# Reciprocal roots of a two-layer encoder trunk: a root on ScalarE and a reciprocal on VectorE instead of logarithm and exponential

## The chip, the cores and the metric

One core of a Trainium2 chip runs the whole program. The metric is the device time of one execution in microseconds. TensorE (PE) multiplies matrices, VectorE (DVE) and ScalarE (ACT) do the elementwise work, GpSimd (POOL) does some of it, and SyncE's queue (SP) issues most of the transfers. ScalarE evaluates its functions from tables; where the next function needs another table, the program has an ACT_TABLE_LOAD instruction on ScalarE ahead of it.

## What is computed

The input is 512 frames of 1024 features. Each of two layers is a SwiGLU block, a mixer block and a second SwiGLU block; one more normalisation ends the trunk. The places that need a reciprocal root are these (the rest of the reference is cut away):

```
_rmsnorm(x, g):              x * rsqrt(mean(x*x) + 1e-6) * g        # ahead of each block, and at the end: 7
_head_standardize(y, eps):   (y - mu) * rsqrt(var + eps)            # eps 64e-5 for RWKV-7, 1e-5 for mLSTM
_rwkv7_mixer:                kk = k * k_k
                             kk = kk / max(sqrt(sum(kk*kk)), 1e-12)
layer:  h += 0.5 * swiglu(rmsnorm(h)) ; h += W_out(sig(g_a) * P_a(rwkv7(xn)) + sig(g_b) * P_b(mlstm(xn)))
        h += 0.5 * swiglu(rmsnorm(h))
```

## The kernel before

Features lie on the 128 partitions and the 512 frames along the free dimension. A product of 32-bit precision is made of three TensorE passes: weights and inputs are split into a rounded high part (on ScalarE, L424 for weights) and a remainder (on VectorE, L425), and lines L460 to L462 multiply high by high, high by low and low by high. Weights stream from memory through SyncE's queue; a tile of 1024 columns is used as two halves of 512.

A SwiGLU block (`ffn`) projects 22 pairs of tiles and then eight output tiles. Its normalisation is not applied to the input: `norm` computes `rstd` from the summed squares `acc` while the first projection runs, and L541 multiplies the product by it afterwards. While the eight output tiles of a block are made, a callback (`spill`, `ready` or, at the end of the program, `scaled`) prepares the next block's input tile by tile and adds its squares to `acc`.

A mixer block (`mixers`) runs under a class `Weave`, which writes out TensorE's order by hand from estimated times: generators for the RWKV-7 heads (four pairs, `rwkv`), the mLSTM heads (four, `mlstm_head`) and the shared projections (`common`) take turns. The order of the instructions on ScalarE, VectorE and GpSimd is made by the scheduler of the framework from its own estimates; each engine then works its own list strictly in order. `common` begins with a projection (`misc`) and the norm; L571 multiplies by `rstd`, and two further products (L926, L930) wait for what comes out of that chain.

The reciprocal root is `rsqrt` (L512 and L513): a logarithm and then an exponential of minus one half of it, both on ScalarE. It is called from `norm` (7 times, 128x512), from `mlstm_head` at L814 (8 times, 128x4) and from `rwkv_gated` (8 times, 128x512, on the tile `gn`, which is `acc`). `rwkv_in` does the same by hand at L957 and L958 (8 times, 128x512): there the sum is first scaled by 65536 inside the logarithm, so the result is a 256th of the root, and the factor of 256 sits in a table of columns `k256` that GpSimd fills near the start. That makes 31 roots. The functions that need a table elsewhere are Silu (L543, SwiGLU), Tanh (which also makes the sigmoids) and Exp in the mixers, and one logarithm per layer at L708. Copies, casts and squares need no table of their own.

Of the kernel before, what the change touches and what calls it, by code (L numbers as in the profile page):

```python
# [11 lines left out]
F32 = mybir.dt.float32  # L12
F32R = mybir.dt.float32r
AF = mybir.ActivationFunctionType
ALU = mybir.AluOpType
# [3 lines left out]
P = 128  # L19
D = 1024  # L20
T = 512
L = 2
FF = 2816
KD = D // P
# [304 lines left out]
class Trunk:  # L329
    def __init__(self, ctx, tc, a, out):  # L330
        self.tc, self.nc, self.a, self.out = tc, tc.nc, a, out
        pool = lambda n, b, **k: ctx.enter_context(tc.tile_pool(name=n, bufs=b, **k))
        self.pw = pool("weights", 3)
        self.pt = pool("tmp", 2)
        self.pmm = pool("mm", 3, space=PSUM)
        self.pmx = pool("mx", 5, space=PSUM)
        self.pd = pool("dram", 1, space=DRAM)
        self.keep = Scope(tc)
        nc = self.nc
        k = self.keep.tile  # L340
        self.xh = k((P, KD, T), F32R, "xh")
        self.xl = k((P, KD, T), F32R, "xl")
        self.rstd = k((P, T), F32, "rstd")
        self.acc = k((P, T), F32, "acc")
        self.cst = k((P, 4, P), F32, "cst")
        self.sel = k((P, 7, P), F32R, "sel")
        self.big = k((P, 512), F32, "big")
        self.fin = k((P, KD), F32, "fin")
        self.tid = k((P, 8, 16), F32, "tid")
        self.vec = [k((P, NCOL), F32, f"vec{l}") for l in range(L)]  # L350
        self.half = [k((P, NCOL), F32, f"half{l}") for l in range(L)]
        self.k256 = [k((P, 4), F32, f"k256_{l}") for l in range(L)]
        self.eps = k((P, 4), F32, "eps")
        self.onemu = [k((P, 15), F32, f"onemu{l}") for l in range(L)]

        k((P, 96), F32, "pad")
        self.sq, self.sl = (k((P, 512), F32R, n) for n in ("sq", "sl"))
        self.ld = [k((P, 512), F32, f"ld{i}") for i in range(2)]
        self.residual()
        for i, e in enumerate((RMS_EPS, GN_EPS, LN_EPS)):  # L360
            nc.gpsimd.memset(self.eps[:, i : i + 1], e)
        nc.scalar.copy(out=self.eps[:, 3:4], in_=self.eps[:, 0:1])
        nc.sync.dma_start(out=self.vec[0], in_=a["vec"][0])
        self.ident = self.cst[:, 0, :]
        dram = lambda n, k, s: [self.pd.tile(s, F32, name=f"{n}{i}", tag=f"{n}{i}") for i in range(k)]
        self.vfirst = dram("vfirst", 4, [P, T])
        self.bonus = dram("bonus", 4, [P, T])
        self.yd = dram("yd", 8, [P, T])
        self.hd = dram("hd", KD, [P, T])
        self.mxd = dram("mxd", 4, [64, 16, 16])  # L370
        self.gd = dram("gd", 16, [P, T])
        self.zd = dram("zd", 4, [P, 8, 16])

    def constants(self):

        nc, a = self.nc, self.a
        nc.sync.dma_start(out=self.vec[1], in_=a["vec"][1])
        nc.sync.dma_start(out=self.big, in_=a["big"])
        nc.sync.dma_start(out=self.fin, in_=a["fin"])
        nc.sync.dma_start(out=self.tid, in_=a["tid"])  # L380
        for l in range(L):
            nc.gpsimd.tensor_scalar(out=self.half[l], in0=self.vec[l], scalar1=0.5, scalar2=None, op0=ALU.mult)
        raw = self.pw.tile([P, KD * P], F32, name="wraw", tag="wraw", bufs=2)
        nc.sync.dma_start(out=raw[:, 0 : 7 * P], in_=a["sel"].rearrange("p a b -> p (a b)"))
        nc.scalar.copy(out=self.sel.rearrange("p a b -> p (a b)"), in_=raw[:, 0 : 7 * P])
        for l in range(L):
            nc.gpsimd.tensor_scalar(out=self.k256[l], in0=self.cols(l, "k_k"), scalar1=256.0, scalar2=None, op0=ALU.mult)
            s0 = _COLS["mu_misc"][0]
            nc.gpsimd.tensor_scalar(out=self.onemu[l], in0=self.vec[l][:, s0 : s0 + 15], scalar1=-1.0, scalar2=1.0, op0=ALU.mult, op1=ALU.add)

# [116 lines left out]
            eng = nc.vector if i == KD - 1 else nc.gpsimd  # L507
            eng.tensor_tensor(out=self.acc, in0=self.acc, in1=sq, op=ALU.add)  # L508

    def rsqrt(self, out, in_, eps, scale=1.0):  # L510
        nc = self.nc
        nc.scalar.activation(out=out, in_=in_, func=AF.Ln, bias=eps, scale=scale)  # L512
        nc.scalar.activation(out=out, in_=out, func=AF.Exp, scale=-0.5)  # L513

    def norm(self, last=None):
        nc = self.nc
        ps = self.mx()
        nc.tensor.matmul(ps, lhsT=self.cst[:, 1, :], rhs=self.acc, start=True, stop=last is None)
        if last is not None:
            nc.tensor.matmul(ps, lhsT=self.cst[:, 1, :], rhs=last, start=False, stop=True)  # L520
        self.rsqrt(self.rstd, ps, self.eps[:, 0:1])

    def ffn(self, l, m, done, first=None):
        nc = self.nc
# [247 lines left out]
    def mlstm_head(self, h):  # L772
        nc, l, wv = self.nc, self.l, self.wv
# [4 lines left out]
        for i in range(4):  # L778
# [4 lines left out]
            ps = self.mx()  # L783
            nc.tensor.matmul(ps[:, :n], lhsT=qk[:, 1, P * i : P * i + P], rhs=qk[:, 0, P * i :], start=True, stop=True)  # L784
            wv.pe(4 * n / 2400.0 + 0.25 * (i == 0))
            p = pt[i]
# [7 lines left out]
        s, hv = self.m_sm, pt[0].rearrange("p (j c) -> p j c", j=4)  # L794
# [16 lines left out]

        nc.vector.tensor_tensor(out=s[:, :, 8:10], in0=s[:, :, 8:10], in1=s[:, :, 1:2].broadcast_to([P, 4, 2]), op=ALU.mult)
        nc.vector.tensor_tensor(out=s[:, :, 9:10], in0=s[:, :, 9:10], in1=s[:, :, 1:2], op=ALU.mult)
        self.rsqrt(s[:, :, 10:11], s[:, :, 9:10], self.eps[:, 2:3])  # L814
        nc.vector.tensor_tensor(out=s[:, :, 1:2], in0=s[:, :, 1:2], in1=s[:, :, 10:11], op=ALU.mult)
        nc.vector.scalar_tensor_tensor(out=s[:, :, 8:9], in0=s[:, :, 8:9], scalar=-1.0, in1=s[:, :, 10:11], op0=ALU.mult, op1=ALU.mult)
        for j in range(4):
# [98 lines left out]
    def rwkv_in(self, p):  # L916

        nc, l, src, mats, wa, zm, wv = self.nc, self.l, self.src, self.mats, self.r_wa, self.zm, self.wv
# [6 lines left out]
        ps = self.mx()  # L925
# [3 lines left out]
        ps = self.mx()  # L929
# [23 lines left out]
        ps = self.sums(0)  # L953
        wv.pe(0.5)
        wv.free("halves")
        nc.vector.tensor_scalar(out=kk, in0=ps, scalar1=1e-24, scalar2=None, op0=ALU.max)
        nc.scalar.activation(out=kk, in_=kk, func=AF.Ln, scale=65536.0)  # L957
        nc.scalar.activation(out=kk, in_=kk, func=AF.Exp, scale=-0.5)  # L958
        self.shifted(rz, "mu_r", p, r)
        nc.vector.scalar_tensor_tensor(out=kk, in0=k, scalar=self.k256[l][:, p : p + 1], in1=kk, op0=ALU.mult, op1=ALU.mult)  # L960
        nc.vector.tensor_tensor(out=a3[:, :, 1:CH], in0=k3[:, :, 1:CH], in1=d3[:, :, 0 : CH - 1], op=ALU.mult)
        nc.gpsimd.tensor_copy(out=a3[:, :, 0:1], in_=k3[:, :, 0:1])
        nc.vector.scalar_tensor_tensor(out=bk[:, :, 0, :], in0=bk[:, :, 0, :], scalar=0.5, in1=k3, op0=ALU.mult, op1=ALU.mult)
# [224 lines left out]
    def rwkv_gated(self, p):  # L1188

        nc, l, mats, sg, gn, wv = self.nc, self.l, self.mats, self.r_sg, self.acc, self.wv  # L1190
        chunks = lambda x: x.rearrange("p (c t) -> p c t", c=NC)
        y = self.r_set[p % 2][0][:, :, 0, :]
        b = self.ld[0]
        nc.sync.dma_start(out=b, in_=self.bonus[p])
        yield "lock", "halves"
        self.halve(y)
        yield "at", wv.mark(2.3, 1.5)
        ps = self.sums(2)
        wv.pe(0.5)
        wv.free("halves")  # L1200
        nc.vector.tensor_tensor(out=y, in0=y, in1=chunks(ps), op=ALU.subtract)
        nc.scalar.activation(out=chunks(gn), in_=y, func=AF.Square)
        yield "lock", "halves"
        self.halve(gn)
        yield "at", wv.mark(3.2, 1.5)
        ps = self.sums(2)
        wv.pe(0.5)
        wv.free("halves")
        self.rsqrt(gn, ps, self.eps[:, 1:2])
        nc.vector.tensor_tensor(out=y, in0=y, in1=chunks(gn), op=ALU.mult)  # L1210
        nc.scalar.activation(out=y, in_=y, func=AF.Identity, scale=self.col(l, "gn_w", p), bias=self.col(l, "gn_b", p))
        nc.gpsimd.tensor_tensor(out=y, in0=y, in1=chunks(b), op=ALU.add)
        yield "at", wv.mark(6.0, 0.8)
        yield "flag", "common"
        ps = self.mx()
        F = slice(P * p, P * p + P)
        nc.tensor.matmul(ps, lhsT=mats[:, 1, F], rhs=sg, start=True, stop=False)
        lw, lx = self.low[0]
        nc.tensor.matmul(ps, lhsT=lw[:, F], rhs=lx, start=False, stop=True)
        nc.vector.tensor_tensor(out=y, in0=chunks(ps), in1=y, op=ALU.mult)  # L1220
        wv.pe(0.7)
        wv.mark(0.7, 0.7)
        nc.sync.dma_start(out=chunks(self.yd[p]), in_=y)

    def run(self):
# [12 lines left out]
        def spill(i, l):  # L1238
            self.feed(i, self.col(l, "gm", i))
            self.squares(i)  # L1240
            nc.sync.dma_start(out=self.hd[i], in_=self.h[:, i, :])

        def ready(i, l, name):
# [3 lines left out]
        def scaled(i):  # L1247

            if i < KD - 1:
                self.squares(i)  # L1250
            else:
                self.last = self.tmp("t1", 1)
                nc.scalar.activation(out=self.last, in_=self.h[:, i, :], func=AF.Square)
            nc.gpsimd.tensor_scalar(out=self.h[:, i, :], in0=self.h[:, i, :], scalar1=self.fin[:, i : i + 1], scalar2=None, op0=ALU.mult)
# [25 lines left out]
```

## Time and profile before

| | |
|---|---|
| time, median of 3 runs | 2444.64 us (2443.34 to 2445.88) |
| the profiled execution: its own time | 2444.26 us |
| its span in the trace | 2442.6 us (1.66 us lie around it) |
| busy: PE / DVE / ACT / POOL | 98% / 54% / 43% / 5% |
| chain of work that ended last: PE / DVE / ACT | 88% / 6% / 3% |
| granted TensorE clock, mean | 0.993 of full speed |
| moved by DMA | 256.13 MB, 105 GB/s on average |

The span runs from the first to the last instruction of the trace. Busy shares are averages over the whole program; PE's share counts matmuls whose ends are modelled, so back-to-back matmuls count as fully busy.

### The profile page before, as it was taken

To read this page: it belongs to the slowest core of one execution; us is meant where nothing else is said; L and a number is where in the kernel's file an instruction comes from. 1 tells how busy PE (TensorE), PEld (TensorE's weight loads), DVE (VectorE), ACT (ScalarE), POOL (GpSimd) and SP (SyncE) were. 2 spreads that over 40 slices of the span, in tenths; PEclk is the share of its full clock that TensorE was granted. 3 is DMA by queue.
4 is the path that set the end of the run, shared out by engine and by line. 5 is a ranking of instruction groups with operands and counts; after the bars stand their busy time and mean duration, and the time that the engine had idled before them with its cause. 6 is when DMAs were issued, how large, how long until landed. Compare 5 with 4: busy or idle time off the path is not lost.

```text
span 2442.6 us, 33611 instructions
## 1 busy us (share of the span) xinstructions
PE 2391.7 (98%) x13140; PEld 1948.9 (80%) x13140; DVE 1307.6 (54%) x2340; ACT 1054.2 (43%) x1795; POOL 112.8 (5%) x151
## 2 busy tenths in 40 slices
PE   8999998999999999999999999989999999999997
PEld 6888887787787888888888888867777878888886
DVE  5444447776766644444444444478677665444333
ACT  5333336555645443333343333365566454333322
POOL 0000010000000100000000000100000001000012
PEclk9999999999999999999999999999999999999999
DMA  4223342322344422323333223423223444222332
GB/s 157 95 97 101 109 121 79 112 75 78 103 151 138 139 95 97 101 93 95 98 97 102 95 93 113 134 71 95 83 87 104 137 150 135 95 95 95 96 99 82
DMA packets 116799, 256.13 MB, mean 105 GB/s; under 512 B 40064, under 2 KB 43264, under 8 KB 116640
## 3 DMA queue, kind: packets, MB, share of 16 engines
q1 hardware_dynamic: 115696, 251.30, 32.8%
q8 instruction: 103, 1.69, 0.3%
q10 hardware_dynamic: 624, 1.64, 0.2%
q0 software_dynamic: 320, 1.05, 0.1%
q14 instruction: 56, 0.46, 0.1%
HBM read 230.88 MB, written 23.07 MB: 104 GB/s over the span
## 4 chain that ended last, share of the span: by engine, by line
PE 88%; DVE 6%; ACT 3%; DMA 1%; issue 1%; SPq 0%; DVEq 0%; ACTq 0%
PE mm L460 27%; PE mm L461 27%; PE mm L462 27%; PE mx L1159 1%; DVE wlo L425 1%; PE mx L676 1%; PE mx L799 1%; PE mx L1147 1%; PE mx L784 0%; PE mx L1178 0%; PE mx L1005 0%; DVE pr L1065 0%; PE mx L1105 0%; ACT L512 0%; DVE tz L1067 0%
## 5 line engine op out<-in xcount | busy, mean ns | idle before, releaser
L424 ACT CAST whi<-wraw 128x512 fp32r<-128x512 f32 (+1 forms) x800 | 486.5, 610 | 1063.7 <-PE mm L461 984.5
L460 PE MATMUL mm<-xh,whi 128*128 128x512 f32 x2160 | 864.5, 400 | 11.2 <-ACT whi L424 11.2
L425 DVE TENSOR_TENSOR wlo<-wraw,whi 128x512 fp32r<-128x512 f32 (+1 forms) x800 | 556.2, 697 | 589.0 <-ACT whi L424 582.6
L462 PE MATMUL mm<-xh,wlo 128*128 128x512 f32 x2160 | 847.0, 392 | 5.3 <-DVE wlo L425 5.2
L461 PE MATMUL mm<-xl,whi 128*128 128x512 f32 x2160 | 845.9, 392 | 0.0
L460 PEld LDWEIGHTS mm<-xh,whi 128*128 128x128 f32 x2160 | 408.1, 189 | 105.1 <-ACT whi L424 12.3
L462 PEld LDWEIGHTS mm<-xh,wlo 128*128 128x128 f32 x2160 | 407.9, 189 | 93.1 <-DVE wlo L425 6.9
L461 PEld LDWEIGHTS mm<-xl,whi 128*128 128x128 f32 x2160 | 408.4, 189 | 82.2 <-issue 1.4
L460 PE MATMUL mm<-hh,whi 128*128 128x512 f32 x704 | 274.2, 390 | 0.0
L462 PE MATMUL mm<-hh,wlo 128*128 128x512 f32 x704 | 274.2, 390 | 0.0
L461 PE MATMUL mm<-hl,whi 128*128 128x512 f32 x704 | 274.2, 390 | 0.0
L461 PEld LDWEIGHTS mm<-hl,whi 128*128 128x128 f32 x704 | 132.3, 188 | 27.4
L462 PEld LDWEIGHTS mm<-hh,wlo 128*128 128x128 f32 x704 | 132.2, 188 | 27.3
L460 PEld LDWEIGHTS mm<-hh,whi 128*128 128x128 f32 x704 | 132.3, 188 | 27.2
L541 DVE TENSOR_TENSOR t<-mm,rstd 128x512 f32<-128x512 f32 x88 | 60.9, 692 | 139.9 <-PE mm L462 127.5
L545 DVE TENSOR_TENSOR t<-mm,t 128x512 f32<-128x512 f32 x88 | 60.9, 692 | 133.0 <-PE mm L462 130.6
L508 POOL TENSOR_TENSOR acc<-acc,t 128x512 f32<-128x512 f32 x36 | 47.9, 1329 | 1187.6 <-ACT t L506 1173.0
L543 ACT ACTIVATE t<-t 128x512 f32<-128x512 f32 x88 | 55.8, 634 | 28.9 <-DVE t L541 28.7
L487 ACT CAST hh<-t 128x512 fp32r<-128x512 f32 x88 | 54.7, 621 | 24.9 <-DVE t L545 24.9
L488 DVE TENSOR_TENSOR hl<-t,hh 128x512 fp32r<-128x512 f32 x88 | 61.0, 693 | 7.6
L495 ACT ACTIVATE xh<-h,vec 128x512 fp32r<-128x512 f32 x48 | 34.5, 724 | 45.1 <-DVE h L557 33.7
L496 DVE SCALAR_TENSOR_TENSOR xl<-h,vec,xh 128x512 fp32r<-128x512 f32 x48 | 35.8, 751 | 28.7 <-ACT xh L495 28.7
(247 smaller groups left out, 2082.7 us busy)
## 6 DMA issues: line engine op xcount, KB each, us to landing
wraw<-wi SPq DMA_DIRECT2D x94, 512.0 KB, 3.5
wraw<-f2i SPq DMA_DIRECT2D x88, 512.0 KB, 3.3
wraw<-f1i SPq DMA_DIRECT2D x86, 512.0 KB, 3.3
wraw<-f1o SPq DMA_DIRECT2D x32, 512.0 KB, 3.6
wraw<-f2o SPq DMA_DIRECT2D x32, 512.0 KB, 3.6
gd<-t SPq DMA_DIRECT2D x32, 256.0 KB, 3.4
wraw<-br SPq DMA_DIRECT2D x32, 256.0 KB, 3.1
wraw<-wo SPq DMA_DIRECT2D x16, 512.0 KB, 3.4
```

What stands on the lines that cost most here:

```text
L424: nc.scalar.copy(out=hi, in_=raw)
L425: nc.vector.tensor_tensor(out=lo, in0=raw, in1=hi.bitcast(F32), op=ALU.subtract)
L460: nc.tensor.matmul(ps, lhsT=hi, rhs=xh, start=first, stop=False)
L461: nc.tensor.matmul(ps, lhsT=hi, rhs=xl, start=False, stop=False)
L462: nc.tensor.matmul(ps, lhsT=lo, rhs=xh, start=False, stop=last)
L487: nc.scalar.copy(out=hi, in_=x)
L488: nc.vector.tensor_tensor(out=lo, in0=x, in1=hi.bitcast(F32), op=ALU.subtract)
L496: nc.vector.scalar_tensor_tensor(out=self.xl[:, i, :], in0=h, scalar=gain, in1=self.xh[:, i, :].bitcast(F32), op0=ALU.mult, op1=ALU.subtract)
L508: eng.tensor_tensor(out=self.acc, in0=self.acc, in1=sq, op=ALU.add)
L541: nc.vector.tensor_tensor(out=g, in0=pg, in1=self.rstd, op=ALU.mult)
L543: nc.scalar.activation(out=s, in_=g, func=AF.Silu)
L545: nc.vector.tensor_tensor(out=p, in0=pu, in1=s, op=ALU.mult)
```

## The change

`rsqrt` goes. A new function `root` takes the root on ScalarE (Sqrt, with the same added constant) and then the reciprocal in place on VectorE. `rwkv_in` does the same by hand, without the factor of 65536, so `k256` and its two GpSimd instructions go and L960 uses the plain column `k_k`; a filler tile grows from 96 to 112 columns. A second new function, `table`, takes the root of one column into a spare column of `eps`; it is called in `spill` (the end of the first SwiGLU block of either layer) and in `scaled` (the end of the last one) right after the squares of the last tile but one. The constant that is added, the shapes and TensorE's order are as before.

```diff
@@ trunk, constants
-        self.k256 = [k((P, 4), F32, f"k256_{l}") for l in range(L)]
-        k((P, 96), F32, "pad")
+        k((P, 112), F32, "pad")
-            nc.gpsimd.tensor_scalar(out=self.k256[l], in0=self.cols(l, "k_k"), scalar1=256.0, scalar2=None, op0=ALU.mult)
@@ rsqrt
-    def rsqrt(self, out, in_, eps, scale=1.0):
-        nc = self.nc
-        nc.scalar.activation(out=out, in_=in_, func=AF.Ln, bias=eps, scale=scale)
-        nc.scalar.activation(out=out, in_=out, func=AF.Exp, scale=-0.5)
+    def table(self):
+
+        self.nc.scalar.activation(out=self.eps[:, 3:4], in_=self.eps[:, 0:1], func=AF.Sqrt)
+
+    def root(self, out, in_, eps):
+        self.nc.scalar.activation(out=out, in_=in_, func=AF.Sqrt, bias=eps)
+        self.nc.vector.reciprocal(out=out, in_=out)
@@ norm, mlstm_head, rwkv_gated
-        self.rsqrt(self.rstd, ps, self.eps[:, 0:1])
+        self.root(self.rstd, ps, self.eps[:, 0:1])
-        self.rsqrt(s[:, :, 10:11], s[:, :, 9:10], self.eps[:, 2:3])
+        self.root(s[:, :, 10:11], s[:, :, 9:10], self.eps[:, 2:3])
-        self.rsqrt(gn, ps, self.eps[:, 1:2])
+        self.root(gn, ps, self.eps[:, 1:2])
@@ rwkv_in
-        nc.scalar.activation(out=kk, in_=kk, func=AF.Ln, scale=65536.0)
-        nc.scalar.activation(out=kk, in_=kk, func=AF.Exp, scale=-0.5)
+        nc.scalar.activation(out=kk, in_=kk, func=AF.Sqrt)
+        nc.vector.reciprocal(out=kk, in_=kk)
         self.shifted(rz, "mu_r", p, r)
-        nc.vector.scalar_tensor_tensor(out=kk, in0=k, scalar=self.k256[l][:, p : p + 1], in1=kk, op0=ALU.mult, op1=ALU.mult)
+        nc.vector.scalar_tensor_tensor(out=kk, in0=k, scalar=self.col(l, "k_k", p), in1=kk, op0=ALU.mult, op1=ALU.mult)
@@ spill, scaled: after self.squares(i)
+            if i == KD - 2:
+                self.table()
```

## Rows read from the trace of the kernel before

**Rows 1.** Page, busy time, share of the span and instructions of each engine.

```profile
PE 2391.7 (98%) x13140; PEld 1948.9 (80%) x13140; DVE 1307.6 (54%) x2340; ACT 1054.2 (43%) x1795; POOL 112.8 (5%) x151
```

**Rows 2.** Busy time by stretch: layer 1 mixer start, rest, SwiGLU; program's end.

```profile
369.00:402.00 33.00, 26.55 (x109) 20.04 (x109) 23.07 (x36) 24.21 (x35) 1.71 (x4) 0.91 0.22 72
402.00:864.00 462.00, 454.71 (x3318) 363.61 (x3317) 317.95 (x673) 249.00 (x452) 25.41 (x42) 0.99 0.36 113
864.00:1224.00 360.00, 360.00 (x1588) 298.01 (x1587) 154.12 (x227) 124.56 (x201) 8.00 (x6) 1.00 0.31 97
2418.00:2442.60 24.60, 10.19 (x41) 7.14 (x39) 7.25 (x8) 4.51 (x5) 4.49 (x3) 0.76 0.23 85
```

**Rows 3.** ScalarE's table loads by line: count, duration ns min/median/max.

```profile
L512 ACT ACT_TABLE_LOAD  x22: 1283/1283/1283, 21.9 to 2428.4; - x22
...
L513 ACT ACT_TABLE_LOAD  x22: 1283/1283/1283, 23.9 to 2430.4; - x22
...
L957 ACT ACT_TABLE_LOAD  x7: 1283/1283/1283, 411.3 to 1885.8; - x7
...
L958 ACT ACT_TABLE_LOAD  x7: 1283/1283/1283, 413.7 to 1888.7; - x7
```

**Rows 4.** VectorE instructions by line: duration ns min/median/max, then shape.

```profile
L806 DVE RECIPROCAL sm<-sm x8: 147/164/166, 466.6 to 1854.9; 128x4 f32<-128x4 f32 x8
...
L882 DVE COPY rcol<-mx x2: 152/152/152, 384.1 to 1593.3; 128x4 f32<-128x4 f32 x2
...
L541 DVE TENSOR_TENSOR t<-mm,rstd x88: 683/692/692, 25.9 to 2301.1; 128x512 f32<-128x512 f32 x88
...
L928 DVE TENSOR_SCALAR rw_w<-rw_w x8: 417/420/427, 394.0 to 1864.0; 128x512 f32<-128x512 f32 x8
...
L937 DVE TENSOR_TENSOR_SCAN rw_w<-big,rw_w x8: 1215/1224/1227, 395.7 to 1864.5; 128x512 f32<-128x512 f32 x8
```

**Rows 5.** Timeline, start of layer 1's mixer: start, duration, engine, line.

```profile
376.09 1.02 PE L518 MATMUL mx<-acc,cst 128*128 128x512 f32 x2
...
378.05 0.69 ACT L512 ACTIVATE rstd<-mx,eps 128x512 f32<-128x512 f32 x1
378.75 1.28 ACT L513 ACT_TABLE_LOAD   x1
380.05 0.63 ACT L513 ACTIVATE rstd<-rstd 128x512 f32<-128x512 f32 x1
...
380.71 0.69 DVE L571 TENSOR_TENSOR zt<-mm,rstd 128x512 f32<-128x512 f32 x1 [3.25 <-ACT rstd L513]
```

**Rows 6.** Timeline, TensorE's waits after the mixer starts, both layers.

```profile
386.88 0.69 PE L926 MATMUL mx<-wa,mats 64*128 64x512 f32 x1 [1.07 <-ACT wa L875]
...
399.81 0.80 PE L462 MATMUL mm<-xh,wlo 128*128 128x512 f32 x1 [4.51 <-DVE wlo L425]
...
1610.35 0.50 PE L460 MATMUL mm<-xh,whi 128*128 128x512 f32 x1 [3.19 <-ACT whi L424]
```

**Rows 7.** Timeline, TensorE's waits inside the mixers, both layers.

```profile
471.20 0.47 PE L1097 MATMUL mx<-mn,u 32*16 32x16 f32 x24 [0.62 <-ACT u L1092]
...
612.33 0.44 PE L676 MATMUL mx<-cst,t 128*128 128x128 f32 x2 [1.53 <-ACT t L753]
...
637.77 0.32 PE L1128 MATMUL mx<-s,mn 64*64 64x64 f32 x2 [1.77 <-ACT s L1039]
638.53 0.69 PE L1128 MATMUL mx<-s,mn 64*64 64x64 f32 x8 [0.44 <-ACT s L1039]
...
1683.77 0.39 PE L1097 MATMUL mx<-mn,u 32*16 32x16 f32 x18 [0.99 <-ACT u L1092]
```

**Rows 8.** Timeline, the end of the program.

```profile
2428.44 1.13 PE L520 MATMUL mx<-t,cst 128*128 128x512 f32 x2 [1.37 <-ACT t L1253]
...
2429.70 0.69 ACT L512 ACTIVATE rstd<-mx,eps 128x512 f32<-128x512 f32 x1
...
2432.43 1.79 DVE L1265 TENSOR_TENSOR h<-h,rstd 128x512 f32<-128x512 f32 x1 [4.76 <-ACT rstd L513]
```

More of the change, by code (lines that the diff above doesn't have):

```diff
@@ L1250, in scaled @@
                 self.squares(i)
+                if i == KD - 2:
+                    self.table()
             else:
```

## The prediction

> **What bounds the kernel now.** I read the page's busy times first: TensorE works 98% of the span [rows 1], so ScalarE and VectorE matter only where TensorE waits for them. The table by stretches says where that can be. In a SwiGLU stretch TensorE is busy for 360.00 of 360.00 us [rows 2]; the other SwiGLU stretches look the same. The four norms that stand ahead of SwiGLU blocks therefore earn nothing, whatever they cost. What is left is three kinds of places: the first 33 us of a mixer (26.55 busy, so 6.45 us lost), the rest of a mixer (7.3 us lost in 462), and the end of the program, where TensorE has finished [rows 2]. Layer 2's mixer looks like layer 1's. I then read the loads by line, and the timelines at these three kinds of places.
>
> **What one root costs now.** Nearly every root brings two table loads, one ahead of the logarithm and one ahead of the exponential: 22 + 22 + 7 + 7 = 58 loads of 1.283 us for 31 roots [rows 3]. A 128x512 root is thus some 3.9 us of ScalarE: load 1.28, logarithm 0.69, load 1.28, exponential 0.63 [rows 5].
>
> **What it costs afterwards.** Sqrt keeps the logarithm's form (one pass over the same PSUM tile with an added column), so I take its 0.69 us [rows 5]. Sqrt needs its own table, and I assume that none of Exp, Tanh or Silu lies in it; otherwise the load count would fall further. So the load ahead of the exponential does not simply vanish: the next Exp or Tanh brings its table back, later. It does vanish ahead of the four Silu blocks (which load a table anyway), at the end, and where a second root follows before any Exp or Tanh, which by ScalarE's present order is six or seven times. About 12 loads go, 15 us of ScalarE, and 23 full exponentials of 0.63 us with 8 small ones, another 16 us.
>
> **The price of the reciprocal** is the weak point, since no 128x512 reciprocal is in the trace. The nearest row is the same instruction on 128x4: 164 ns [rows 4]. A copy of 128x4 takes 152 ns. Lower bound: the cheapest 128x512 form seen, 0.42 us (L928). Upper bound: if the 12 ns above the copy all come from its four elements, each costs 3 ns more than an ordinary one. An ordinary one costs (692 - 152) / 508 = 1.06 ns, so 512 elements take 0.15 + 512 x 4.06 ns = 2.2 us. I take 0.69 us, the common price of 128x512 (L541), because at four elements the reciprocal stands within 8% of a plain copy. VectorE then gains 23 x 0.69 + 8 x 0.16 = 17 us over 1307.6 [rows 1], which is harmless as a share.
>
> The Trainium skill speaks against the change here: the page "VectorE: DVE Perf Modes", section "First, the fixed hardware budget", says that the reciprocal runs on iterative divide operations with a repeat count of 8. If that means eight cycles for each element, the change makes the kernel slower; the rival below works this out from rows. The 128x4 row speaks against that reading, though weakly, since 4 elements are few.
>
> **The start of a mixer, twice.** The norm's matmul ends at 376.09 + 1.02 = 377.11; the logarithm begins only at 378.05, because its load stands in front of it; L571, the first user of `rstd`, begins at 380.71 [rows 5]. With the table loaded during the SwiGLU stretch before (where TensorE never waits, so that 1.3 us load is covered), Sqrt begins about 0.1 us after the matmul, at 377.21, and ends at 377.90; the reciprocal ends at about 378.6, and L571 follows. That is 2.1 us earlier: 0.84 from the load moved away, 1.28 from the second load and the shorter second step. The Exp table must then come back ahead of the first Tanh (L886), but ScalarE has gaps there while VectorE makes that Tanh's input, so I charge nothing; uncovered it would cost up to 1.3. TensorE's waits after this are for the chain out of `rstd`: 1.07 us at L926, and then 4.51 us at a weight remainder which queues on VectorE behind that chain; in layer 2, 3.19 us at a weight cast [rows 6]. These ends all move with `rstd`. I count the whole 2.1 us, twice: -4.2.
>
> **The end, once.** The last matmul of the norm ends at 2428.44 + 1.13 = 2429.57, and the logarithm begins at 2429.70 [rows 8]: here the first load is almost hidden behind the matmul already, so loading it early gives no more than 0.05. From the logarithm's start to L1265 are 2.73 us; Sqrt and reciprocal take 1.38. Gain 1.4 us, all on the path: -1.4.
>
> **Inside the mixers.** I went through the waits of TensorE and kept those whose releaser stood on ScalarE right behind a root's exponential or its load. L1092 stood behind one in either layer: 0.62 and 0.99 us, saved whole. L1039 waited behind the pair of loads of a `gn` root: 1.77 + 0.44, of which I save 2.0. L753 stood behind L958: 1.53 in each layer, of which the product it copies explains all but 0.86, so 1.7 for both [rows 7]. Together 5.3 us saved. Against that stand the returning loads. The waits just listed add up to 6.9 us for 58 loads, 0.12 us a load. About twenty loads (31 roots, less the five ahead of a Silu or the end, less six or seven that another root follows) now stand at new places, ahead of some Exp or Tanh: 20 x 0.12 = 2.4 us lost. VectorE's extra 0.69 us in front of L960 and L1210 replaces an exponential and a load of which it used to wait for both, so it delays nobody further. What queues behind a reciprocal that waits is weight remainders (L425); they already queue behind L960 and L1210 in the same way. Net -2.9, by far the least certain term; its bounds are -5.3 and +3 (nothing saved, the new places cost a little more than the estimate).
>
> **Nothing for the rest.** The two `k256` instructions go from GpSimd, which is 5% busy [rows 1]. The filler keeps later tiles at their addresses. No transfer moves, and no queue is passed.
>
> **The sum.** -4.2 - 1.4 - 2.9 = -8.5 us against the profiled execution's own 2444.3 (span 2442.6 plus 1.7 around it), which is 0.4 us below the median of the runs shown. That gives 2435.8, and I say 2436 us, 0.35% faster. A difference of about 0.2% (4.9 us) is what a measurement of this kernel can tell from no change.
>
> **Rivals.**
> *A slow reciprocal* (slower). If each element passes eight times at 1.06 ns, 128x512 takes 0.15 + 4.34, about 4.5 us. Each of the three exposed places loses 3.8 us in full, and each of the 16 roots inside the mixers blocks VectorE, which is 69% busy there [rows 2], for as long; TensorE would feel a quarter to a half of that. The loss is 3.8 x (3 + 4) to 3.8 x (3 + 8), or 27 to 42 us, against the 8.5 gained: 2462 to 2478, say 2470. By the larger share the change breaks even at 0.69 + 8.5 / 11 = 1.5 us for a reciprocal; a scan, the slowest 128x512 form seen, takes 1.22 [rows 4], still under it. Chance 0.15. At the upper bound of 2.2 us it would come to some 2452.
> *The gain is eaten.* ScalarE's and VectorE's orders are made anew by the scheduler, and a returning load, or a weight cast placed behind it, can stop TensorE anywhere in 920 us of mixer. If the inner term comes to 0 or +3 and one start gives only half, the time is 2440 to 2443, up to 2447 with bad luck. For it: every waiting place in rows 7 came from just such a chance meeting. Against it: ScalarE has 31 us less to do. Chance 0.18, of which 0.02 still ends as faster, 0.11 as the same and 0.05 as slower.
> *The early load buys nothing* is a part of that: if a later Tanh or Exp were scheduled between the early Sqrt and the norm, each start would give 1.3 instead of 2.1, and the sum 2437.5.
>
> **Chances and range.** The forecast has 0.64, with its own range of 2431 to 2439.7; the gain eaten 0.18; the slow reciprocal 0.15; 0.03 is left for a reciprocal between 1 and 2.2 us, of which 0.02 ends as the same and 0.01 as slower. Faster 0.64 + 0.02 = 0.66, same 0.11 + 0.02 = 0.13, slower 0.15 + 0.05 + 0.01 = 0.21. The range of 2431 to 2452 holds the forecast, the gain eaten and the upper bound of the reciprocal; it leaves out the slow reciprocal and a little at the low end.
>
> **What the next profile would show.** RECIPROCAL 128x512 near 0.69 us; above 1.5 the forecast falls. Some 12 table loads fewer in all, and none between the last square and the last Sqrt. From the norm's matmul to L571's successor some 1.5 us instead of 3.6, and the two stretches at the mixers' starts 2 us shorter. From the last norm matmul's end to the first final multiplication 1.5 instead of 2.9. The SwiGLU stretches unchanged. What would make this wrong is a new TensorE wait inside the mixers released by a ScalarE instruction right behind a table load, or by a VectorE one behind a reciprocal.

## The result, and the profile after

The changed kernel takes 2471.65 us (median of 4 runs, 2470.91 to 2472.9) against 2445.11 us for the kernel before in the same session (2443.34 to 2445.88): a ratio of 1.011, 95% interval 1.0095 to 1.0125. It is 26.5 us slower; 2436 was forecast, with a range up to 2452. The rival called a slow reciprocal had been put at 2470.

The page of the changed kernel, busy time, then two groups of TensorE with the idle time just before them and what ended it; behind these, the same two groups in the kernel before (L460 and L462 there are L458 and L460 here):

```profile
PE 2402.9 (97%) x13140; PEld 1950.9 (79%) x13140; DVE 1380.3 (56%) x2371; ACT 1032.7 (42%) x1758; POOL 110.7 (4%) x149
...
L458 PE MATMUL mm<-xh,whi 128*128 128x512 f32 x2160 | 865.8, 401 | 9.2 <-ACT whi L422 9.2
L460 PE MATMUL mm<-xh,wlo 128*128 128x512 f32 x2160 | 849.2, 393 | 20.0 <-DVE wlo L423 20.0
...
L460 PE MATMUL mm<-xh,whi 128*128 128x512 f32 x2160 | 864.5, 400 | 11.2 <-ACT whi L424 11.2
L462 PE MATMUL mm<-xh,wlo 128*128 128x512 f32 x2160 | 847.0, 392 | 5.3 <-DVE wlo L425 5.2
```

The span is 2469.2 us. Against [rows 1] ScalarE is 21.5 us less busy, where 31 had been reckoned, and VectorE 72.7 us more, where 17 had been reckoned. TensorE executes the same 13140 matmuls, yet is 11.2 us longer busy and (2469.2 - 2402.9) - (2442.6 - 2391.7) = 15.4 us longer idle; the two make up the 26.6 us by which the span grew. The largest part of the new idle time is waiting for weight remainders, 20.0 us instead of 5.2.

The reciprocals by line, duration in ns as min/median/max:

```profile
L514 DVE RECIPROCAL sm<-sm x8: 124/171/181, 471.1 to 1886.3; 128x4 f32<-128x4 f32 x8
L514 DVE RECIPROCAL acc<-acc x8: 3344/3352/3353, 583.2 to 2012.8; 128x512 f32<-128x512 f32 x8
L514 DVE RECIPROCAL rstd<-rstd x7: 3353/3353/3354, 23.5 to 2455.6; 128x512 f32<-128x512 f32 x7
...
L959 DVE RECIPROCAL rw_kk<-rw_kk x8: 3352/3353/3354, 411.4 to 1910.9; 128x512 f32<-128x512 f32 x8
```

A reciprocal of 128x512 takes 3.35 us; the forecast had 0.69, and at most 2.2.

The start of layer 1's mixer, timelines of ScalarE and VectorE; it answers to [rows 5]:

```profile
377.02 1.28 ACT L513 ACT_TABLE_LOAD   x1
378.32 0.69 ACT L513 ACTIVATE rstd<-mx,eps 128x512 f32<-128x512 f32 x1
...
379.04 3.35 DVE L514 RECIPROCAL rstd<-rstd 128x512 f32<-128x512 f32 x1 [1.31 <-ACT rstd L513]
382.31 0.63 DVE L423 TENSOR_TENSOR wlo<-wraw,whi 128x512 fp32r<-128x512 f32 x1
382.85 1.28 DVE L572 TENSOR_TENSOR zt<-mm,rstd 128x512 f32<-128x512 f32 x2
```

VectorE's first use of `rstd` starts at 382.85 instead of 380.71. The reader also sees what should not be there: a load stands right ahead of the Sqrt. ScalarE's rows for the new early roots say why:

```profile
L510 ACT ACTIVATE eps<-eps x3: 203/203/203, 3.6 to 4.1; 128x1 f32<-128x1 f32 x3
L510 ACT ACT_TABLE_LOAD  x1: 1283/1283/1283, 2.3 to 2.3; - x1
```

All three early roots run at 3.6 to 4.1 us, at the start of the program. They read only a constant and write a spare column, so nothing holds them at their places in the text, and the scheduler took them first. The early load was therefore never made at a mixer.

How the loss arises inside a mixer is seen at the first `kk` of layer 1. VectorE, in order of its queue:

```profile
411.42 3.35 DVE L959 RECIPROCAL rw_kk<-rw_kk 128x512 f32<-128x512 f32 x1 [0.54 <-ACT rw_kk L958]
414.69 0.63 DVE L740 TENSOR_TENSOR zt<-mm,rstd 128x512 f32<-128x512 f32 x1
415.24 0.74 DVE L961 SCALAR_TENSOR_TENSOR rw_kk<-rw_k,vec,rw_kk 128x512 f32<-128x512 f32 x1
...
422.61 1.88 DVE L423 TENSOR_TENSOR wlo<-wraw,whi 128x512 fp32r<-128x512 f32 x3
```

The same stretch of VectorE's queue in the kernel before, where L425 makes the remainders and L960 is the first user of the root:

```profile
413.75 0.69 DVE L425 TENSOR_TENSOR wlo<-wraw,whi 128x512 fp32r<-128x512 f32 x1 [1.38 <-ACT whi L424]
415.69 0.75 DVE L960 SCALAR_TENSOR_TENSOR rw_kk<-rw_k,k,rw_kk 128x512 f32<-128x512 f32 x1 [1.25 <-ACT rw_kk L958]
...
423.67 0.69 DVE L425 TENSOR_TENSOR wlo<-wraw,whi 128x512 fp32r<-128x512 f32 x1
```

And TensorE of the changed kernel at that moment:

```profile
423.34 0.75 PE L460 MATMUL mm<-xh,wlo 128*128 128x512 f32 x1 [4.23 <-DVE wlo L423]
423.89 0.63 PE L458 MATMUL mm<-xh,whi 128*128 128x512 f32 x1
424.31 0.63 PE L459 MATMUL mm<-xl,whi 128*128 128x512 f32 x1
...
427.10 0.39 PE L460 MATMUL mm<-xh,wlo 128*128 128x512 f32 x1
427.32 0.39 PE L458 MATMUL mm<-xh,whi 128*128 128x512 f32 x1
```

The weight remainder that TensorE needs at 419.1 sits in VectorE's queue behind the reciprocal and the thirteen instructions after it. Counted from the program's start, the remainder made at 422.61 is the same one that the kernel before made at 413.75, in a pause of VectorE ahead of L960. It comes 8.9 us later because the scheduler placed it behind the reciprocal and the thirteen instructions, which take 3.35 and 7.8 us, instead of ahead of them. Before the change TensorE was busy for all of the 5 us from 418 to 423. And the wait is not all: for the next 3 us a matmul lasts 0.63 us instead of 0.39, and one starts every 0.42 us instead of every 0.22. Busy time by stretch, where the number after the five engines is the granted clock; first the changed kernel, then the kernel before:

```profile
418.00:423.00 5.00, 1.10 (x5) 0.56 (x4) 5.00 (x9) 3.40 (x5) 0.00 (x0) 1.00 0.01 2
423.00:428.00 5.00, 4.66 (x13) 3.71 (x14) 4.00 (x8) 1.07 (x2) 0.00 (x0) 0.66 0.47 143
...
418.00:423.00 5.00, 5.00 (x24) 4.14 (x23) 5.00 (x9) 1.77 (x3) 0.00 (x0) 1.00 0.00 0
423.00:428.00 5.00, 4.87 (x44) 3.71 (x43) 5.00 (x10) 1.50 (x3) 0.00 (x0) 1.00 0.57 160
```

After a wait of 4.23 us the granted clock averages 0.66 over the next 5 us, a stretch that is partly at the lower of the two levels, 1.2 GHz, and partly at 2.4 GHz. Before the change the last of these two stretches had 1.00. Over the whole trace TensorE is busy for 29.6 us at the lower level, against 16.4 before. By the spacing of the matmuls above, about half of the 13.2 us more is lost, some 6 of the 11.2 us of extra busy time; where the rest comes from was not traced.

### The profile page after: what moved, and what is told of

It is laid out like the page before. It is cut to its first block, busy times and chain, and to the rows that moved or that the text cites. A ratio compares the mean times of both kernels' runs of the same rounds, so it can differ in the third digit from the quotient of the medians.

```text
span 2469.2 us, 33626 instructions
## 1 busy us (share of the span) xinstructions
PE 2402.9 (97%) x13140; PEld 1950.9 (79%) x13140; DVE 1380.3 (56%) x2371; ACT 1032.7 (42%) x1758; POOL 110.7 (4%) x149
## 4 chain that ended last, share of the span: by engine, by line
PE 86%; DVE 7%; ACT 3%; DMA 2%; issue 1%; DVEq 0%; SPq 0%; POOL 0%; ACTq 0%; POOLq 0%
PE mm L458 27%; PE mm L460 26%; PE mm L459 26%; DVE wlo L423 1%; PE mx L677 1%; PE mx L1160 1%; DVE pr L1066 0%; PE mx L1179 0%; DMA wraw<-br 0%; DVE tz L1068 0%; DVE qk L745 0%; DVE rw_kk L959 0%; DVE acc L514 0%; PE mx L1006 0%; ACT whi L422 0%
## 5 line engine op out<-in xcount | busy, mean ns | idle before, releaser
L458 PE MATMUL mm<-xh,whi 128*128 128x512 f32 x2160 | 865.8, 401 | 9.2 <-ACT whi L422 9.2
L460 PE MATMUL mm<-xh,wlo 128*128 128x512 f32 x2160 | 849.2, 393 | 20.0 <-DVE wlo L423 20.0
L460 PEld LDWEIGHTS mm<-xh,wlo 128*128 128x128 f32 x2160 | 408.6, 189 | 111.2 <-DVE wlo L423 24.1
L458 PEld LDWEIGHTS mm<-xh,whi 128*128 128x128 f32 x2160 | 409.3, 190 | 104.2 <-ACT whi L422 9.6
L458 PE MATMUL mm<-hh,whi 128*128 128x512 f32 x704 | 273.9, 389 | 0.0
L460 PE MATMUL mm<-hh,wlo 128*128 128x512 f32 x704 | 273.9, 389 | 0.0
L460 PEld LDWEIGHTS mm<-hh,wlo 128*128 128x128 f32 x704 | 132.1, 188 | 27.5
L458 PEld LDWEIGHTS mm<-hh,whi 128*128 128x128 f32 x704 | 132.1, 188 | 27.3
L494 DVE SCALAR_TENSOR_TENSOR xl<-h,vec,xh 128x512 fp32r<-128x512 f32 x48 | 35.8, 751 | 29.6 <-ACT xh L493 29.6
```

Of the source, the lines that this page charges most:

```text
L458: nc.tensor.matmul(ps, lhsT=hi, rhs=xh, start=first, stop=False)
L460: nc.tensor.matmul(ps, lhsT=lo, rhs=xh, start=False, stop=last)
L494: nc.vector.scalar_tensor_tensor(out=self.xl[:, i, :], in0=h, scalar=gain, in1=self.xh[:, i, :].bitcast(F32), op0=ALU.mult, op1=ALU.subtract)
```

## Experiments

Theory 1: the loss is the time that a 128x512 reciprocal holds VectorE. Theory 2: it is the table loads at new places and the new order on the engines. (The scheduler makes its order anew for each kernel, so no run here changes the reciprocals and leaves the order as it was.) Each kernel was timed beside the kernel before on the same chip.

**An ordinary instruction in the reciprocal's place** (`cheap_step`).

```diff
-        self.nc.scalar.activation(out=out, in_=in_, func=AF.Sqrt, bias=eps)
-        self.nc.vector.reciprocal(out=out, in_=out)
+        self.nc.scalar.activation(out=out, in_=in_, func=AF.Sqrt, bias=eps, scale=0.0)
+        if len(out.shape) == 3:
+            self.nc.vector.reciprocal(out=out, in_=out)
+        else:
+            self.nc.vector.tensor_tensor(out=out, in0=out, in1=out, op=ALU.min)
...
-        nc.vector.reciprocal(out=kk, in_=kk)
+        nc.vector.tensor_tensor(out=kk, in0=kk, in1=kk, op=ALU.subtract)
```

> The changed kernel with each of the 23 reciprocals of 128x512 replaced by an elementwise minimum of the tile with itself, an ordinary 128x512 VectorE instruction of some 0.69 us (the roots are also scaled to constants, so the outputs are not the reference's; ScalarE's functions and table loads are kept, and so are the 128x4 reciprocals). Theory 1, the loss is the 3.35 us that a 128x512 reciprocal holds VectorE: the loss vanishes, 2436 to 2445 us. Theory 2, the loss is the table loads at new places and the new order of the engines: it stays, above 2460 us.

At `kk` the stand-in was a subtraction of the tile from itself. Measured: 2433.53 us against 2445.29, ratio 0.9952 (0.9935 to 0.9969). The stand-in takes what the forecast had charged for the reciprocal:

```profile
L517 DVE TENSOR_TENSOR acc<-acc 128x512 f32<-128x512 f32 x8 | 5.5, 689 | 4.0 <-ACT acc L513 3.7
```

So with a step of ordinary price in the reciprocal's place the kernel is 11.8 us faster than before, and below the range of theory 1. The 2.66 us more that each of 23 reciprocals takes are worth 38 us, together with the order that the scheduler makes around them: here the remainder of the example above is made right behind the stand-in.

```profile
413.18 0.69 DVE L962 TENSOR_TENSOR rw_kk<-rw_kk 128x512 f32<-128x512 f32 x1 [0.88 <-ACT rw_kk L961]
413.78 0.69 DVE L423 TENSOR_TENSOR wlo<-wraw,whi 128x512 fp32r<-128x512 f32 x1
```

Theory 1 holds so far that without the slow instruction there is no loss; by theory 2 a loss would have stayed, with 56 table loads here and 58 in the changed kernel. How the 38 us divide between the time held and the order around it is not shown.

**Both steps** (`both_steps`): the kernel before with its two loads kept, the exponential giving the root, and a reciprocal behind it (in `rwkv_in` the same by hand).

```diff
-        nc.scalar.activation(out=out, in_=out, func=AF.Exp, scale=-0.5)
+        nc.scalar.activation(out=out, in_=out, func=AF.Exp, scale=0.5)
+        nc.vector.reciprocal(out=out, in_=out)
```

> The kernel before, with its logarithm and exponential and both table loads kept (the exponential now gives the root), and a reciprocal on VectorE added behind each, 31 in all. Theory 1: each of the 23 large ones adds 3.35 us to VectorE and to its chain with nothing taken from ScalarE, so the time is that of the changed kernel or more, 2468 to 2490 us. Theory 2: tables and ScalarE's work are as before, so 2445 to 2452 us.

Measured: 2519.42 us, ratio 1.0306 (1.029 to 1.0321), 74 us more. Theory 1, and well above its range: 23 x 3.35 = 77 us of reciprocals come out almost undiminished in the time, though 4 of the 23 stand ahead of SwiGLU blocks.

**One place at a time** (`only_norm`, `only_kk`, `only_gn`, `only_small`): the kernel before, with `root` at one kind of place and the logarithm and exponential at the others, without early loads. For `only_norm`:

```diff
-        self.rsqrt(self.rstd, ps, self.eps[:, 0:1])
+        self.root(self.rstd, ps, self.eps[:, 0:1])
```

> The kernel before with Sqrt and reciprocal in the 7 norms alone, no early load. Theory 1: only three of the seven places are exposed (two mixer starts and the end), where the chain becomes about 3.35 - 0.63 - 1.28 = 1.4 us longer, plus weight remainders that queue behind the reciprocal: 2448 to 2454 us. Theory 2: three Silu loads fewer to change and few new places, 2443 to 2447 us.

Measured: 2445.21 us, ratio 0.9999 (0.999 to 1.0008). Seven norms cost nothing in sum, less than theory 1 had reckoned. In the trace the end of the program does lose 1.4 us, but the two mixers come out 2.6 us shorter together, though VectorE uses `rstd` 1.8 us later there; why was not traced.

> The kernel before with Sqrt and reciprocal at the 8 normalisations of kk alone. Theory 1: VectorE is held for 3.35 us eight times inside the mixers, with weight remainders queued behind; about half of the inner loss, 2452 to 2460 us. Theory 2: loads move at 8 of 31 places, within 4 us of the kernel before, 2442 to 2449 us.

Measured: 2460.18 us, ratio 1.0064 (1.0049 to 1.0079), just past the upper end of theory 1.

> The kernel before with Sqrt and reciprocal at the 8 roots of gn alone. The change as a whole costs 26.5 us, the 8 at kk alone cost 15 and the 7 norms nothing. Theory 1a, the loss is a sum over the places where VectorE is held: 8 to 13 us here, 2453 to 2458. Theory 1b, the places meet (one reciprocal queues behind another, or behind the remainders that the other delayed): under 7 us here, 2445 to 2452, the rest being their product.

Measured: 2464.48 us against 2445.53, ratio 1.0078 (1.0063 to 1.0093), beyond both theories.

> The kernel before with Sqrt and reciprocal at the 8 mLSTM roots of 128x4 alone. Theory 1: a reciprocal of 0.17 us holds nobody, and an exponential and some loads go: 2440 to 2445 us. Theory 2, the returning loads cost: 2446 to 2452. Were the parts of the change to add up (norms 0, kk 15, gn 19, all of it 26.5), this one would have to save 7.5 us: 2438.

Measured: 2452.22 us against 2446.01, ratio 1.0034 (1.0021 to 1.0047). Here theory 2 was right: 8 reciprocals of 0.17 us cannot cost 6 us. ScalarE's timeline at the first mLSTM head of this kernel shows what does, and TensorE's wait behind it:

```profile
467.14 1.28 ACT L516 ACT_TABLE_LOAD   x1
468.45 0.30 ACT L516 ACTIVATE sm<-sm,eps 128x4 f32<-128x4 f32 x1
468.77 1.28 ACT L961 ACT_TABLE_LOAD   x1
470.06 0.63 ACT L961 ACTIVATE rw_kk<-rw_kk 128x512 f32<-128x512 f32 x1
...
472.11 1.28 ACT L962 ACT_TABLE_LOAD   x1
...
474.44 0.97 PE L1101 MATMUL mx<-mn,u 32*16 32x16 f32 x64 [2.98 <-ACT u L1096]
```

The same place in the kernel before:

```profile
466.25 1.28 ACT L512 ACT_TABLE_LOAD   x1
...
468.63 0.63 ACT L957 ACTIVATE rw_kk<-rw_kk 128x512 f32<-128x512 f32 x1 [0.77 <-DVE rw_kk L956]
469.28 1.28 ACT L513 ACT_TABLE_LOAD   x1
```

Two roots meet here. Before, both logarithms shared one load and both exponentials another; now Sqrt, logarithm and exponential need three. TensorE's wait is 2.98 us where it was 0.62 [rows 7]; its twin in layer 2 went from 0.99 to 3.70. The four parts, -0.1, 14.9, 19.0 and 6.2 us, add up to 40 and not to 26.5. At the place shown a kernel with roots of both kinds pays for a third table, which the whole change does not. The number of loads does not explain the sum, though: over all lines it is 67 before and 58 with the whole change, 69 with `kk` alone or the small roots alone, but 65 with `gn` alone, the dearest part, and 62 with the norms alone. What makes the parts dearer than the whole stays open.

**The reciprocal in four pieces** (`pieces`).

```diff
-        self.nc.vector.reciprocal(out=out, in_=out)
+        if len(out.shape) == 3:
+            self.nc.vector.reciprocal(out=out, in_=out)
+        else:
+            for j in range(4):
+                self.nc.vector.reciprocal(out=out[:, P * j : P * j + P], in_=out[:, P * j : P * j + P])
```

> The changed kernel with each 128x512 reciprocal cut into four of 128x128 (some 0.95 us each, 3.8 us in all). Theory 1a, TensorE waits because weight remainders queue behind a whole reciprocal: a remainder can now slip in between two pieces, so much of the loss goes, 2450 to 2465 us. Theory 1b, TensorE waits for the chain behind the root and for VectorE's sum: nothing is won and 0.4 us per root is lost, 2471 to 2482 us.

Measured: 2473.65 us, ratio 1.0115 (1.01 to 1.0131), in the range of theory 1b. This told nothing of what it was made for: in 22 of 23 places the scheduler kept the four pieces together, as here, so no remainder could slip in.

```profile
411.55 3.39 DVE L964 RECIPROCAL rw_kk<-rw_kk 128x128 f32<-128x128 f32 x4 [0.49 <-ACT rw_kk L962]
414.86 0.63 DVE L744 TENSOR_TENSOR zt<-mm,rstd 128x512 f32<-128x512 f32 x1
```

**VectorE held, no chain longer** (`held`): the kernel before, with reciprocals on tiles that nobody reads any more.

```diff
         nc.vector.tensor_tensor(out=r, in0=r, in1=d3, op=ALU.mult)
+        nc.vector.reciprocal(out=kk, in_=kk)
...
         nc.vector.tensor_tensor(out=y, in0=y, in1=chunks(gn), op=ALU.mult)
+        nc.vector.reciprocal(out=gn, in_=gn)
```

> The kernel before, with logarithms and exponentials as they are, and a reciprocal in place on tiles that nobody reads any more: on kk after the last instruction that uses it, and on gn after its multiplication, 16 of 128x512 in all. VectorE is held for 16 x 3.35 us, but no root's chain is longer. Theory 1a, TensorE waits for what queues on VectorE behind a reciprocal: 20 to 40 us more, 2465 to 2485. Theory 1b, it waits because the chain from a root to its users is longer: less than 8 us more, 2445 to 2453.

Measured: 2506.14 us, ratio 1.0255 (1.0239 to 1.027), 60 us more for 16 x 3.35 = 54 us of reciprocals that nobody waits for by data. The two longest groups of TensorE's waits in this kernel, in us, times, longest:

```profile
PE mm L462 <- DVE wlo L425: 28.5, 11, 5.9
PE mm L460 <- ACT whi L424: 11.4, 3, 7.3
```

The longest group is again the weight remainders in VectorE's queue. A longer chain behind a root is not needed for a loss; theory 1b falls, and theory 1a had put the loss at 40 us at most. Of the 64.5 us by which the span grew, 36.6 are idle time and 27.9 longer busy time, with TensorE busy for 63.2 us at the lower clock level against 16.4. Why 16 reciprocals cost more here than 23 in the change was not tested; the scheduler's order differs here too.

**The early load held back** (`after_early`, and `cheap_early` on top of `cheap_step`): `table` reads a column of the summed squares, so it cannot run before they exist.

```diff
-        self.nc.scalar.activation(out=self.eps[:, 3:4], in_=self.eps[:, 0:1], func=AF.Sqrt)
+        self.nc.scalar.activation(out=self.eps[:, 3:4], in_=self.acc[:, 0:1], func=AF.Sqrt)
```

> The changed kernel with the early Sqrt reading a column of the summed squares, so that the scheduler can't place it before those exist. Theory of the prediction: both Sqrt at the mixer starts then begin within 0.2 us of the norm's matmul instead of 0.9 after it, and the end gains nothing: 1.5 us less in all, 2469 to 2471.5 us. Rival: the scheduler finds another order and the time moves by several us either way, or the table is lost again to a function placed in between.

Measured: 2474.87 us, ratio 1.0122 (1.0107 to 1.0138): 3 us more than the change where 1.5 less was expected, so the rival holds here. The early load itself did what was meant: the three early roots run at 362.8, 1582.8 and 2445.5 us, and at the first mixer the Sqrt begins 0.04 us after the norm's matmul instead of 0.94. TensorE's waits at the start of layer 1's mixer, first in the changed kernel, then here:

```profile
389.06 1.04 PE L927 MATMUL mx<-wa,mats 64*128 64x512 f32 x1 [2.99 <-ACT wa L876]
...
388.16 0.69 PE L927 MATMUL mx<-wa,mats 64*128 64x512 f32 x1 [1.03 <-ACT wa L876]
...
400.69 0.50 PE L458 MATMUL mm<-xh,whi 128*128 128x512 f32 x1 [3.03 <-ACT whi L422]
```

The wait for the chain out of `rstd` shrinks by 2 us. But in each mixer the scheduler also placed a weight cast later in ScalarE's queue, and TensorE now waits for one.

> The kernel cheap_step (an ordinary 128x512 VectorE instruction of 0.69 us in place of the reciprocal, roots scaled to constants, so the outputs are not the reference's) with the early load held back until the squares exist. This is the kernel that the prediction added up: 2436 us by it, 2432 by the measured cheap_step less 1.7 for two mixer starts. If early loads do not earn: 2433 to 2436.

Measured: 2429.27 us, ratio 0.994 (0.9926 to 0.9955), 4.3 us less than `cheap_step` without it and below both forecasts.

**Root and reciprocal in one ScalarE function** (`one_step`, `one_step_late`): the changed kernel with ScalarE's function for the reciprocal root of the absolute value in place of Sqrt and reciprocal. VectorE has nothing to do for a root; in `one_step` the early load is placed as in `after_early`.

```diff
     def root(self, out, in_, eps):
-        self.nc.scalar.activation(out=out, in_=in_, func=AF.Sqrt, bias=eps)
-        self.nc.vector.reciprocal(out=out, in_=out)
+        self.nc.scalar.activation(out=out, in_=in_, func=AF.Abs_reciprocal_sqrt, bias=eps)
```

`rwkv_in` and `table` use the same function.

> [...] Theory 1: the loss is all in the reciprocal, so this is at or below the kernel with the ordinary VectorE step, 2428 to 2435 us. Theory 2: table loads are as in the changed kernel, above 2445 us.

Measured: 2425.96 us against 2445.53, ratio 0.9923 (0.9907 to 0.994). This is below the range of theory 1. This version beats both kernels, by 19.6 us and 46 us; how exact the function is was not measured here. Its start of layer 1's mixer, to be read against [rows 5]:

```profile
377.24 0.69 ACT L513 ACTIVATE rstd<-mx,eps 128x512 f32<-128x512 f32 x1 [0.41 <-PE mx L518]
...
377.96 0.69 DVE L571 TENSOR_TENSOR zt<-mm,rstd 128x512 f32<-128x512 f32 x1 [0.41 <-ACT rstd L513]
```

No load stands ahead of the root any more, and VectorE uses `rstd` 0.72 us after the root began, where it was 2.66.

> The kernel one_step with the early loads written as in the change, without an input that holds them back, so that all three run at the very start of the program. If the early loads earn what the prediction said, two mixer starts lose 0.85 us each and the end nothing: 1 to 2 us more than one_step, 2426 to 2430. If they only shift the scheduler's order: a difference of either sign, up to 4 us.

Measured: 2433.24 us, ratio 0.9954 (0.9937 to 0.9971): without an early load that takes effect it is 7.3 us slower by the medians, several times what two mixer starts were reckoned at (the two intervals touch). With 3.2 us the wrong way in `after_early`, what an early load is worth in the time can't be told from the reordering that comes with it.

## Why the prediction was wrong, step by step

**What bounds the kernel** was right. The SwiGLU stretch shows TensorE busy throughout, as in [rows 2] (busy time by stretch of the changed kernel):

```profile
402.00:864.00 462.00, 446.73 (x3266) 354.00 (x3266) 339.48 (x682) 241.33 (x435) 23.46 (x41) 0.99 0.36 110
864.00:1224.00 360.00, 360.00 (x1588) 297.71 (x1587) 156.57 (x227) 121.92 (x198) 9.34 (x7) 1.00 0.31 97
```

Measured in the traces from the end of one norm's matmul to that of the next, the SwiGLU stretch is as long as before, layer 1's mixer 8.2 us longer, layer 2's 16.7, and all that follows it 1.5: nearly the whole loss lies in the mixers, and twice as much in the second. That `only_norm` comes out at 0.9999 fits with it only in part: four of its seven reciprocals stand ahead of SwiGLU blocks, while of the three exposed places the end loses and the mixers gain.

**The price of the reciprocal** is the step that failed. The prediction took 0.69 us and bounded it by 2.2 from a 128x4 reciprocal that stood 12 ns above a copy. Measured are 3.35 us: (3353 - 171) / 508 = 6.3 ns for each element, six times the 1.06 ns of an ordinary instruction [rows 4]. With it comes the sign that the prediction had named for being wrong, a new wait of TensorE behind a reciprocal (4.23 us at 423.34). The bound was built badly. Four elements at 6.3 ns are 25 ns in an instruction of 171 ns, and the time of so short an instruction varies by as much (the 128x4 reciprocals run from 147 to 166 ns before [rows 4] and from 124 to 181 at L514). The difference of two fixed parts was read as a price per element and multiplied by 512. The page "VectorE: DVE Perf Modes" of the Trainium skill, section "First, the fixed hardware budget", gives the reciprocal a repeat count of 8. Read as eight passes for each element, as in the rival, that has the direction right; the trace has about six times an ordinary element, not eight.

**VectorE's extra time "delays nobody further"** hung on that price. At 0.69 us it is not contradicted: in `cheap_step` TensorE waits 4.7 us for weight remainders, where it was 5.2 before. At 3.35 us it is wrong. `held` shows that holding VectorE can cost TensorE more than the time held, through the weight remainders behind it and the clock after each wait; the rival had given 0.25 to 0.5 for each us inside the mixers. From `cheap_step` to the change, 38 us of loss stand for 2.66 us x 19 exposed reciprocals = 50.5 us, three quarters. A straight line between these two kernels breaks even at 0.69 + 2.66 x 11.8 / 38.1 = 1.5 us for a reciprocal, the point that the rival had named. Its 2470 was close by luck: a price too high (4.5 us) met a share too low.

**Two tables for a root**, of which the second comes back later, was right in kind: by the sums over the lines the loads went from 67 to 58, nine fewer where about 12 were reckoned.

**The start of a mixer** was right about the chain and wrong about the waits. In `cheap_early`, which has the early load and a step of 0.69 us, VectorE uses `rstd` 1.49 us after the norm's matmul; 1.5 was forecast. But TensorE's waits, which were to end earlier with `rstd`, follow the order of ScalarE's and VectorE's lists. In layer 1 of `cheap_early` the wait of 1.07 us [rows 6] has become 3.84, behind two table loads:

```profile
387.69 1.28 ACT L879 ACT_TABLE_LOAD   x1
...
389.67 0.72 PE L930 MATMUL mx<-wa,mats 64*128 64x512 f32 x1 [3.84 <-ACT wa L879]
```

In layer 2 the wait for a weight cast has gone from 3.19 to 7.42 us. The 4.51 us at a weight remainder are gone in the changed kernel, where `rstd` comes later, and in `cheap_step`, where it comes 1.2 us earlier, they are still 4.52. Counting the whole 2.1 us twice was not borne out. (The 1.28 us put down to the second load and a "shorter second step" are the load alone: 0.69 us was reckoned where the exponential takes 0.63.)

**The early load** was not made where the text puts it; the prediction had considered that a table might be lost in between, but not that the load would move to the beginning.

**The gains** were real, but the sum that gave them is not confirmed. With an ordinary price and the early load held back, the kernel that the prediction added up to 2436 took 2429.27, a gain of 16.7 us instead of 8.5. Between the two profiled executions 11.4 us lie in layer 1's mixer, 2.7 in layer 2's and 1.3 behind it, where the terms gave 3.5 for either mixer and 1.4 for the end. At the end of the program the terms hold: from the root's start to the first multiplication on VectorE the changed kernel has 4.17 us, which is the forecast's 1.38 with 2.66 for the slower reciprocal and 0.13 over:

```profile
2454.90 0.69 ACT L513 ACTIVATE rstd<-mx,eps 128x512 f32<-128x512 f32 x1
...
2455.62 3.35 DVE L514 RECIPROCAL rstd<-rstd 128x512 f32<-128x512 f32 x1 [2.76 <-ACT rstd L513]
2459.07 5.87 DVE L1270 TENSOR_TENSOR h<-h,rstd 128x512 f32<-128x512 f32 x6
```

What stays open is how the extra gain divides between removed waits and the scheduler's new order; the early load's different signs suggest that the order alone is worth several us. That a remainder let in between two pieces of a reciprocal would save much was not shown, since the pieces stayed together.

## What to carry to other kernels

A price read from a tiny tile is a price of the fixed part: before an instruction is scaled up by a hundred, measure it at full width, and if that can't be done, let the forecast rest on the rival as much. Where one engine also prepares what the bounding engine eats next, a slow instruction on it can cost most of its length or more, whatever that engine's busy share says; how much depends on what the scheduler places behind it. And an instruction that is to warm something up needs an input that exists only then, or a scheduler may run it at once, as it did here.

## What the runs showed of the hardware that was not expected

A reciprocal on VectorE costs 6.3 ns for each element of a partition against 1.06 for an ordinary instruction: 0.17 us for 128x4 and 3.35 us for 128x512, and the four pieces of 128x128 took 3.39 us together. A wait of TensorE of 4.23 us was followed by some 3 us in which matmuls took 0.63 us instead of 0.39, with a granted clock of 0.66 over 5 us, so this wait cost more than its length. Of the 26.6 us that the span grew, 11.2 are longer busy time of the same matmuls, some 6 of them at the lower clock level. ScalarE's single function for the reciprocal root took the same 0.69 us as Sqrt or the logarithm.
